# W2's product in the seven-product form, and the weight sums chained by adding DMA transfers

## The chip, the cores and the metric

One core of a Trainium2 chip. The metric is device time in microseconds of one execution; the median of the runs shown counts.

## What is computed

One layer of an encoder over 768 tokens (512 of one request, 256 of the other), in float32: a half-step SwiGLU FFN, a mixer (attention and two-way HGRN2 side by side), and a second half-step FFN, each followed by a residual and a layer norm. The change touches the two FFNs and the loads of weights everywhere.

```python
def swiglu_ffn(x, w13, w2):                    # x 768 x 1024, w13 1024 x 5632, w2 2816 x 1024
    gate, up = jnp.split(x @ w13, 2, axis=-1)
    return (jax.nn.silu(gate) * up) @ w2
...
x = layer_norm(ALPHA * x + 0.5 * swiglu_ffn(x, ffn_w13[l, 0], ffn_w2[l, 0]), ln_g[l, 0], ln_b[l, 0])
```

## The kernel before

**Numbers in two parts.** Every operand of a large product is split into a high part, rounded to the matmul's format by a ScalarE cast (L112), and the rest, by a VectorE subtraction (L113). A product is the sum of three passes, high x high, high x low, low x high (`PASSES`, L144).

**The FFN** runs 11 steps (`ffn`, loop at L504). A step makes two tiles of 128 hidden columns: gate products, up products, SiLU and their product H. W13's products are already in a seven-product form (Strassen-Winograd): activations and weights are cut into 2 x 2 blocks, seven products of block sums replace eight, and sums of the results give the four output blocks. `pair_products` (L371) does the seven products B11, B21, T2, T1, T3, B22, T4 in this order, each 4 x 3 matmuls of 384 columns. The activations' block sums are made once and stay in SBUF (`areaA`, `areaB`); the weights' sums are made for every pair.

**The weights of a pair.** `pair_loads` (L331) loads three blocks in one transfer and two in another, and adds a block A21 onto the latter two by transfers that GpSimd issues with `accum_op=ALU.add` (L340; "adding transfer" here). `pair_weights` (L343) makes two more sums on VectorE (L359) and splits seven blocks into `ring` tiles, of which there are six; so a weight can be split when an earlier product has left its ring tile.

**W2.** Steps 1 to 9 also multiply the H of the step before by two rows of tiles of W2: `group` (L443) takes one token tile and one half of W2's columns, 2 x 3 matmuls of 512 columns into a PSUM tile `pd` (two of them), and VectorE adds the result to the residual `xr` (L452). Twelve such groups are a step's share; `fill` (L510) puts one behind each product from the third on. The last two steps' H goes through `group` after the loop, with the layer norm behind it (`finish`, L533). `w2_units` (L431) loads and splits W2.

**Order.** The framework puts each engine's instructions in order at build time, by the program's order and by when it expects operands, buffers and banks to be ready, and adds the waits. SP issues plain loads, GpSimd adding transfers and a few tiny instructions of the layer norms. Buffers have names with a size and a count (`BUFS`, L77): an allocation waits for an earlier user of the same name.

**First steps.** `first_a` (L550) starts the first FFN from a transposed copy of x, `first_pairs` (L463) the second; both do the first gate pair by plain products and then the first up pair's weights and the activations' sums. `load` and `unit` (L121, L134) load W_in and W_out between the FFNs in tiles of 128 x 1024.

Of the kernel before, what the change touches and what calls it, by code (L numbers as in the profile page):

```python
# [14 lines left out]
P = 128  # L15
# [23 lines left out]
def encoder_layer(ctx: ExitStack, tc: tile.TileContext, a, y_prompt, y_sample):  # L39
# [30 lines left out]
    def area_b(n, dt):  # L70
# [7 lines left out]
            "Dt": (768, 1), "P1": (768, 1), "Ft": (1536, 1), "qt": (768, 1), "nr": (384, 1), "Dc": (192, 1),  # L78
            "xb": (1536, 2)}
# [38 lines left out]
    def raw_tile():  # L118
        return wp.tile([P, 1024], F32, name="raw", tag="raw", bufs=4)

    def load(*srcs):  # L121

        raw = raw_tile()
        if len(srcs[0].shape) == 2:
            nc.sync.dma_start(raw, srcs[0])
            return raw
        r3 = raw.rearrange("p (k c) -> p k c", k=srcs[0].shape[1])
        c0 = 0
        for s in srcs:
            nc.sync.dma_start(r3[:, :, c0:c0 + s.shape[2]], s)  # L130
            c0 += s.shape[2]
        return raw

    def unit(*srcs, hl=None):  # L134

        raw = load(*srcs)
        hl = hl or (ring(), ring())
        split(hl[0], hl[1], raw)
        return hl
# [6 lines left out]
    CHUNK = 8  # L146

# [48 lines left out]
    def constants():  # L196

        k = {}

        rows = raw_tile()[:24, :P]  # L200
# [28 lines left out]
        mraw = raw_tile()  # L229
# [101 lines left out]
    def pair_loads(idx, j):  # L331


        w = a["w13_t"][idx, j]
        base = buf("xb").rearrange("p (b k c) -> p b k c", b=3, k=4)
        nc.sync.dma_start(base, w[:, :3])
        sums = raw_tile().rearrange("p (b k c) -> p b k c", b=2, k=4)
        nc.sync.dma_start(sums, w[:, :2])
        for b in range(2):
            nc.gpsimd.dma_start(sums[:, b], w[:, 3], accum_op=ALU.add)  # L340
        return [base[:, b] for b in range(3)] + [sums[:, b] for b in range(2)]

    def pair_weights(r, slots=()):  # L343


        A22, A11, A12, S1, S3 = r
        slots = list(slots)
        out = []
        S = {}

        def put(src):
            rg = (slots.pop(0) if slots else None) or ring()
            v = rg.rearrange("p (s k c) -> p s k c", s=2, k=4)
            split(v[:, 0], v[:, 1], src)
            out.append(v)

        def add(tag, x, y):
            t_ = buf(tag, n=512).rearrange("p (k c) -> p k c", k=4)
            dve.tensor_tensor(t_, x, y, ALU.add)  # L359
            return t_  # L360

        def s2():
            S[2] = add("Dt", S1, A11)
            put(S[2])

        def s4():
            put(add("P1", S[2], A12))

        return [lambda: put(A11), lambda: put(A12), s2, lambda: put(S1), lambda: put(S3), s4, lambda: put(A22)], out

    def pair_products(ws, C, fill, par):  # L371
# [7 lines left out]
        def product(b, bank, more=False):  # L379
            n = 0  # L380
            tl, off, dist = spot(b)
            for k in range(4):
                for wi, xi in PASSES:
                    pe.matmul(bank, lhsT=ws[b][:, wi, k, :],  # L384
                              rhs=view(tl, off + xi * 512 + k * P, [[dist, 3], [1, P]]),
                              start=n == 0 and not more, stop=n == 11, skip_group_check=True)
                    n += 1
            fill(b)
# [17 lines left out]
    BLOCK = ((1, 2), (3, 0))  # L406
    W2R = ("kc", "kc", "P2", "Xt")
    ORD = (1, 2, 0, 2, 1, 0, 2, 0, 2, 0, 2)

    def ffn(idx, ln_idx, tail, first):  # L410
# [11 lines left out]
        def up_pair(ws, G, hs, fill):  # L422
# [5 lines left out]
            for j in range(2):  # L428
                split(hs[j][:, :T], hs[j][:, T:], H[:, j, :])

        def w2_units(s, last=False):  # L431

            raws = [load(w2[f * P:(f + 1) * P, :]) for f in (2 * s, 2 * s + 1)]
            out = [[], []]
            for c in range(2):
                for j in range(2):
                    rg = buf(W2R[c * 2 + j], F32R, 1024) if not last else \
                        view(B[2], c * 1024, [[1, 1024]]) if j else view(B[1], 3072 + c * 1024, [[1, 1024]])
                    split(rg[:, :512], rg[:, 512:], raws[j][:, c * 512:(c + 1) * 512])
# [15 lines left out]

        def weights(n):

            do, out = pair_weights(pair_loads(idx, (n % 2) * NS + n // 2))
            for f in do:
                f()  # L460
            return out

        def first_pairs(start):  # L463
# [19 lines left out]
            r = [raw_tile().rearrange("p (m k c) -> p m k c", m=2, k=4) for _ in range(2)]  # L483
            for n in range(2):
                for m in range(2):
                    nc.sync.dma_start(r[n][:, m], a["w13_t"][idx, 0][:, BLOCK[m][n]])
            ru = pair_loads(idx, NS)
            for b, raw in zip((B11, B21), r):
                start(b)
                hl.append([ring().rearrange("p (m k c) -> p m k c", m=2, k=4) for _ in range(2)])  # L490
                split(*hl[-1], raw)
            do, ws = pair_weights(ru, [None, None] + [buf(n, F32R, 1024) for n in W2R])
# [5 lines left out]
            for f in (do[0], do[1], sums[0], do[2], sums[1], do[3], sums[2], do[4], do[5], sums[3], do[6]):  # L498
                f()
            return G, ws  # L500

        G, ws = first(idx, NS) if idx == 0 else first_pairs(first)
        w2l = {}
        for s in range(NS):  # L504
            if s > 0:
                w2l[s - 1] = w2_units(s - 1)
                wg, ws = ws, weights(2 * s + 1)
            todo = [(c, t) for c in range(2) for t in range(NT)] if 0 < s < NS - 1 else []

            def fill(n, s=s, todo=todo):  # L510
                if todo and n >= 0:
                    c, t = todo.pop(0)
                    group([2 * s - 2, 2 * s - 1], w2l[s - 1][c], t, c)

            if s > 0:
                G = gate_pair(wg, lambda n: fill(n - 2))
# [8 lines left out]
            up_pair(wu, G, hs, fill)  # L525
# [4 lines left out]
        bc = ln_rows(ln_idx, raw_tile)  # L530
# [19 lines left out]
    def first_a(idx, ns):  # L550
# [14 lines left out]
        ru = pair_loads(idx, ns)  # L565
        nc.sync.dma_start(ident, a["c_ident"])
        for t in range(NT):
            nc.sync.dma_start(xr[:, t, :], x_rows[t])
# [10 lines left out]
        do, ws = pair_weights(ru, [None, None] + [buf(n, F32R, 1024) for n in W2R])  # L579
        for n in range(2):  # L580
# [16 lines left out]
            if n:  # L597
                do[0]()
                do[1]()
            for m in range(2):  # L600
                act.activation(G[:, m, n * 384:(n + 1) * 384], banks[m], AF.Silu)
        b11, b21, b12, b22 = xb

# [9 lines left out]
        do[2]()  # L613
        do[3]()
        sums(T1, b11)
        do[4]()
        sums(T3, b12)
        do[5]()
        do[6]()
# [382 lines left out]
    def out_unit(k, *places):  # L1002
        raw = load(w_out[k * P:(k + 1) * P, :])
        if not isinstance(places[0], list):
            split(places[0], places[1], raw)
            return [[p_[:, c * 512:(c + 1) * 512] for c in range(2)] for p_ in places]
        for c in range(2):
            split(places[0][c], places[1][c], raw[:, c * 512:(c + 1) * 512])
# [136 lines left out]
```

## Time and profile before

| | us |
|---|---|
| median of 3 runs | 1476.99 (1476.22 to 1478.14) |
| the profiled execution | 1475.67 |
| its span, first to last instruction | 1473.7 |
| TensorE, VectorE, ScalarE, GpSimd busy | 1443.5, 954.1, 615.0, 121.5 |

The rows further down are of the profiled execution. PE is TensorE's matmuls, PEld its weight loads, DVE VectorE, ACT ScalarE, POOL GpSimd, SP the engine that issues plain transfers. In a row of a timeline stand start, duration, engine, line, operation, output<-inputs, shapes and count, and in brackets the idle time before it with what ended it. Matmuls overlap, so their pace is read from starts.

### The profile page before, as it was taken

The numbers are of one execution on the slowest core, as the hardware profiler recorded it, in microseconds if no ns is written. First come the engines' busy times: TensorE is split into PE (matmuls) and PEld (weight loads), VectorE is DVE, ScalarE is ACT, GpSimd is POOL, SyncE is SP. The second block draws the span as 40 slices with busy tenths as digits, with TensorE's granted clock in tenths as the row PEclk, the third lists the DMA queues.
The fourth block names the chain that finished last, engine by engine and source line by source line (L and its number), as shares of the span: only waits on it lengthen the run. The fifth ranks groups of instructions, "written<-read, shape, count | busy, mean of one in ns | idle before, by whom it ended". The sixth has DMA issues, their size and how long they took to land.

```text
span 1473.7 us, 23217 instructions
## 1 busy us (share of the span) xinstructions
PE 1443.5 (98%) x9343; PEld 1338.0 (91%) x9343; DVE 954.1 (65%) x1615; ACT 615.0 (42%) x1222; POOL 121.5 (8%) x149
## 2 busy tenths in 40 slices
PE   7999999999999999999999999999999999999996
PEld 6999999999999898999988987899999999999995
DVE  6866566666666768444588736776666666666656
ACT  7533333333333444465664432363333333333341
POOL 1100000000000110000000002120000000000002
PEclk9999999999999999999999999999999999999999
DMA  9543344342442441111111143142443424434212
GB/s 319 156 115 99 95 114 111 98 108 86 115 113 95 126 115 44 58 30 30 44 30 45 32 143 114 43 115 65 115 110 98 109 85 115 112 98 125 67 43 86
DMA packets 67437, 140.80 MB, mean 96 GB/s; under 512 B 13417, under 2 KB 33793, under 8 KB 67329
## 3 DMA queue, kind: packets, MB, share of 16 engines
q1 hardware_dynamic: 55232, 117.29, 23.0%
q0 software_dynamic: 12096, 22.03, 9.6%
q8 instruction: 73, 1.20, 0.3%
q14 instruction: 36, 0.29, 0.1%
HBM read 133.01 MB, written 6.29 MB: 95 GB/s over the span
## 4 chain that ended last, share of the span: by engine, by line
PE 88%; DVE 5%; ACT 2%; DMA 2%; POOL 1%; issue 1%; SPq 0%; DVEq 0%; ACTq 0%; POOLq 0%
PE pa L384 30%; PE pd L448 21%; PE pb L384 12%; PE pa L159 9%; PE ptm L672 4%; PE pwo L1028 4%; PE pp L907 2%; DMA raw<-w_t 1%; PE pav L801 1%; DVE xr L320 1%; DVE Ut L768 1%; PE ps L891 1%; ACT Ft L302 1%; PE ptr L187 1%; PE pp L901 1%
## 5 line engine op out<-in xcount | busy, mean ns | idle before, releaser
L384 PE MATMUL pa<-areaA,ring 128*128 128x384 f32 x1488 | 273.1, 335 | 0.0
L384 PEld LDWEIGHTS pa<-areaA,ring 128*128 128x128 f32 x1488 | 261.0, 188 | 6.0
L448 PE MATMUL pd<-kc,Kt 128*128 128x512 f32 x720 | 185.5, 392 | 0.0
L384 PE MATMUL pa<-areaB,ring 128*128 128x384 f32 x984 | 185.3, 337 | 0.0
L384 PEld LDWEIGHTS pa<-areaB,ring 128*128 128x128 f32 x984 | 174.0, 188 | 6.0
L112 ACT CAST ring<-raw 128x512 fp32r<-128x512 f32 (+2 forms) x116 | 84.6, 731 | 218.7 <-PE pb L384 92.5
L452 DVE SCALAR_TENSOR_TENSOR xr<-pd,xr 128x512 f32<-128x512 f32 x240 | 164.9, 687 | 6.7 <-PE pd L448 6.4
L159 PE MATMUL pa<-areaA,ring 128*128 128x384 f32 x864 | 167.5, 343 | 0.9 <-ACT Kt L691 0.9
L448 PEld LDWEIGHTS pd<-kc,Kt 128*128 128x128 f32 x720 | 133.6, 188 | 21.2
L112 ACT CAST ring<-xb 128x512 fp32r<-128x512 f32 x126 | 77.9, 621 | 176.3 <-PE pa L384 130.1
L159 PEld LDWEIGHTS pa<-areaA,ring 128*128 128x128 f32 x864 | 148.4, 188 | 2.5 <-ACT Kt L691 1.4
L113 DVE TENSOR_TENSOR ring<-xb,ring 128x512 fp32r<-128x512 f32 x126 | 87.6, 698 | 92.7 <-ACT ring L112 90.2
L340 POOL DMA_DIRECT2D raw<-w_t x84 | 74.4, 1038 | 792.4 <-DVE P L359 615.9
L113 DVE TENSOR_TENSOR ring<-raw,ring 128x512 fp32r<-128x512 f32 (+2 forms) x116 | 96.0, 829 | 40.6 <-ACT ring L112 33.8
L448 PE MATMUL pd<-P,Kt 128*128 128x512 f32 x360 | 103.1, 394 | 1.0 <-DVE xr L452 1.0
L448 PE MATMUL pd<-Xt,Kt 128*128 128x512 f32 x360 | 102.4, 392 | 0.0
L384 PE MATMUL pb<-areaB,ring 128*128 128x384 f32 x480 | 91.3, 338 | 0.0
L384 PE MATMUL pb<-areaA,ring 128*128 128x384 f32 x480 | 90.1, 334 | 0.0
L384 PEld LDWEIGHTS pb<-areaB,ring 128*128 128x128 f32 x480 | 85.6, 188 | 3.1
L384 PEld LDWEIGHTS pb<-areaA,ring 128*128 128x128 f32 x480 | 84.5, 188 | 3.4
L672 PE MATMUL ptm<-ring,areaA 128*128 128x256 f32 x576 | 81.7, 289 | 0.0
L448 PEld LDWEIGHTS pd<-Xt,Kt 128*128 128x128 f32 x360 | 67.6, 188 | 15.1
(241 smaller groups left out, 1982.2 us busy)
## 6 DMA issues: line engine op xcount, KB each, us to landing
xb<-w_t SPq DMA_DIRECT2D x42, 768.0 KB, 6.4
raw<-ffn_w SPq DMA_DIRECT2D x44, 512.0 KB, 7.4
raw<-w_t SPq DMA_DIRECT2D x42, 512.0 KB, 3.8
raw<-w_t POOLq DMA_DIRECT2D x84, 256.0 KB, 5.6
raw<-w_in SPq DMA_DIRECT2D x22, 512.0 KB, 3.9
raw<-w_out SPq DMA_DIRECT2D x8, 512.0 KB, 3.4
park<-xr SPq DMA_DIRECT2D x6, 512.0 KB, 3.0
xr<-park SPq DMA_DIRECT2D x6, 512.0 KB, 6.0
```

Of the source, the lines that this page charges most:

```text
L112: act.copy(dst_hi, src)
L113: dve.tensor_tensor(dst_lo, src, dst_hi.bitcast(F32), ALU.subtract)
L159: pe.matmul(pt, lhsT=hl[wi][:, k * P:(k + 1) * P], rhs=tri(g * 2048 + xi * 1024 + k * P), start=n == 0, stop=n == 3 * KT - 1)
L187: pe.transpose(pt[:, k * P:(k + 1) * P], src[:, k * P:(k + 1) * P], ident)
L302: act.activation(junk[c], x[c], AF.Square, bias=nm, accum_out=w[:, 2 + c:3 + c])
L340: nc.gpsimd.dma_start(sums[:, b], w[:, 3], accum_op=ALU.add)
L384: pe.matmul(bank, lhsT=ws[b][:, wi, k, :], rhs=view(tl, off + xi * 512 + k * P, [[dist, 3], [1, P]]), start=n == 0 and not more, stop=n == ...
L448: pe.matmul(pd, lhsT=hT[f][:, hi * T + t * P:hi * T + (t + 1) * P], rhs=w[wi], start=n == 0, stop=n == tot - 1)
L452: dve.scalar_tensor_tensor(xs, pd, 0.5, xs, ALU.mult, ALU.add, accum_out=total)
L672: pe.matmul(pt, lhsT=xT(t, xi, k), rhs=w[k // 4][wi][:, k % 4, :], start=n == 0, stop=n == 3 * KT - 1)
L907: pe.matmul(pp[j][:, 384:448], lhsT=PTs[j % 2][:, i * P:(i + 1) * P], rhs=V[:, kb0 + i, kv * 64:kv * 64 + 64], start=i == 0, stop=i == nk - 1)
L1028: pe.matmul(po[c], lhsT=cat(t, xi, k), rhs=wo[k][wi][c], start=k == 0 and n == 0, stop=k == KT - 1 and n == 2)
```

## The change

For steps 1 to 9 of each FFN the product of H and W2 takes the seven-product form too. H's two tiles and two halves of the tokens are its 2 x 2 blocks, so a product is one block of 128 hidden columns by 384 tokens, times a block of 128 rows and 512 columns of W2 (or sums of such). `h_form` makes H's sums on VectorE (three instructions) and splits seven blocks. `form_groups` runs the products token tile by token tile, three matmuls each. Products of one chain accumulate in the same PSUM tile, and after each the tile is added to or subtracted from the part of `xr` to which its running sum belongs. The 21 groups of a step are taken from `SEQUENCE` behind the products of W13 by the counts in `FILLS`.

Weights of all forms, W13's and W2's, are loaded in blocks of 128 x 512 (`block`, 15 of them, in place of `raw` and `xb`). One sum (S1) is made by an adding transfer at once. The others come one after the other in the block X: it is split as A11, then a transfer adds A21 and it is split as T3, then A22 for T2, then A12 for B22. Only the first up pair of each FFN makes these three on VectorE (`by_dma=False`). The order of the weights of a pair is B11, T3, B21, T2, T1, B22, T4.

Besides: W_in and W_out are loaded and split in two halves; the layer norm's rows go to `Ut` tiles; in `first_a` the first weights are loaded into `xr` and the rows of x after them.

```diff
-            "xb": (1536, 2)}
...
+    BLOCKS = 15
...
+    def form_loads(A11, A12, A21, A22):
+        out = []
+        for src in (A11, A22, A12, A22):
+            t_ = block()
+            nc.sync.dma_start(t_, src)
+            out.append(t_)
+        nc.gpsimd.dma_start(out[1], A21, accum_op=ALU.add)
+        return out, (A21, A22, A12)
+
+    def form_weights(loaded, place, by_dma=True):
+        (X, S1, A12, A22), more = loaded
+        out = [None] * 7
+        def put(n, src):
+            rg = place(n)
+            out[n] = rg[:, :512], rg[:, 512:1024]
+            split(*out[n], src)
+        def thunk(n, src, then=None):
+            def f():
+                put(n, src)
+                if then is not None and by_dma:
+                    nc.gpsimd.dma_start(X, more[then], accum_op=ALU.add)
+            return f
...
+        if by_dma:
+            return {n: thunk(n, src, then) for n, src, then in (
+                (B11, X, 0), (T3, X, 1), (B21, A12, None), (T2, X, 2), (T1, S1, None), (B22, X, None),
+                (T4, A22, None))}, out
+        R = block()
+        nc.sync.dma_start(R, more[0])
...
-        return [lambda: put(A11), lambda: put(A12), s2, lambda: put(S1), lambda: put(S3), s4, lambda: put(A22)], out
...
+    FILLS = (0, 0, 1, 2, 2, 2, 2, 2, 2, 2, 2, 2, 1, 1)
...
+        def h_form(H, G, hs):
...
+            base(B11, 0, 0)
+            dve.tensor_tensor(view(G, 0, [[384, 2], [1, 384]]), view(H, 0, [[1152, 2], [1, 384]]),
+                              view(H, 384, [[0, 2], [1, 384]]), ALU.subtract)
+            dve.scalar_tensor_tensor(G[:, 1, :384], G[:, 0, :384], -1.0, H[:, 1, 384:], ALU.mult, ALU.subtract)
+            dve.scalar_tensor_tensor(G[:, 1, 384:], G[:, 1, :384], -1.0, H[:, 1, :384], ALU.mult, ALU.subtract)
+            sums((T2, T4), buf("Dt", F32R), buf("P1", F32R), G[:, 1, :])
+            ft = buf("Ft", F32R)
+            sums((T1, T3), ft[:, :T], ft[:, T:], G[:, 0, :])
+            base(B21, 1, 0)
+            base(B22, 1, 1)
...
+        W2AT = {B11: "kc", T2: "kc", T3: "P2", T4: "Xt", B21: "kc", T1: "kc", B22: "P2"}
+        C11, C12, C21, C22 = (0, 0, 0.5), (0, 1, 0.5), (1, 0, -0.5), (1, 1, -0.5)
+        CHAINS = ([(B11, [C11]), (T2, [C12]), (T3, [C22]), (T4, [C21])],
+                  [(T1, [C22]), (B22, [C12])], [(B21, [C11])])
+        SEQUENCE = [(0, i, n) for n in range(4) for i in range(2)] + [(0, 2, n) for n in range(4)] + \
+                   [(1, i, n) for n in range(2) for i in range(2)] + [(1, 2, n) for n in range(2)] + \
+                   [(2, i, 0) for i in range(3)]
+        def form_groups(h, do, ws):
+            banks = {}
+            def group(c, i, n):
+                b, outs = CHAINS[c][n]
+                for need in (T3, b) if b == T2 else (b,):
+                    if ws[need] is None:
+                        do[need]()
+                if n == 0:
+                    banks[c, i] = psd("pd")
+                pd = banks[c, i]
+                for m, (hi, wi) in enumerate(PASSES):
+                    pe.matmul(pd, lhsT=h[b][hi][:, i * P:(i + 1) * P], rhs=ws[b][wi],
+                              start=n == 0 and m == 0, stop=m == 2, skip_group_check=True)
+                for half, tok, sign in outs:
+                    xs = xr[:, tok * 3 + i, half * 512:(half + 1) * 512]
+                    dve.scalar_tensor_tensor(xs, pd, sign, xs, ALU.mult, ALU.add)
...
+        ORDER = (B11, T3, B21, T2, T1, B22, T4)
...
             if s > 0:
-                w2l[s - 1] = w2_units(s - 1)
                 wg, ws = ws, weights(2 * s + 1)
...
+                if s < NS - 1:
+                    todo += form_groups(hf, *form_weights(w2_loads(s - 1), lambda b: buf(W2AT[b], F32R, 1024)))
...
-        bc = ln_rows(ln_idx, raw_tile)
+        bc = ln_rows(ln_idx, lambda: buf("Ut", n=1024))
...
-        rw = [raw_tile().rearrange("p (m k c) -> p m k c", m=2, k=4) for _ in range(2)]
+        rw = [xr[:, n, :].rearrange("p (m k c) -> p m k c", m=2, k=4) for n in range(2)]
```

## Rows read from the trace of the kernel before

**Rows 1.** The page's parts 1 and 4: busy us per engine, shares of the chain.

```profile
PE 1443.5 (98%) x9343; PEld 1338.0 (91%) x9343; DVE 954.1 (65%) x1615; ACT 615.0 (42%) x1222; POOL 121.5 (8%) x149
...
PE 88%; DVE 5%; ACT 2%; DMA 2%; POOL 1%; issue 1%; SPq 0%; DVEq 0%; ACTq 0%; POOLq 0%
```

**Rows 2.** Windows: length; PE, PEld, DVE, ACT, POOL busy; clock, DMA share, GB/s.

```profile
223.10:269.02 45.92, 45.92 (x242) 42.86 (x241) 29.25 (x46) 16.30 (x29) 3.54 (x4) 1.00 0.37 103
1024.36:1070.28 45.92, 45.92 (x242) 42.87 (x241) 29.25 (x46) 16.30 (x29) 3.52 (x4) 1.00 0.37 104
```

**Rows 3.** Timeline of TensorE inside one step.

```profile
241.03 2.24 PE L384 MATMUL pa<-areaB,ring 128*128 128x384 f32 x12
243.11 1.55 PE L448 MATMUL pd<-kc,Kt 128*128 128x512 f32 x6
244.51 2.29 PE L384 MATMUL pb<-areaB,ring 128*128 128x384 f32 x12
```

**Rows 4.** Timeline of TensorE in step 1 of the first FFN.

```profile
52.07 0.39 PE L448 MATMUL pd<-kc,Kt 128*128 128x512 f32 x1
52.30 0.87 PE L384 MATMUL pb<-areaA,ring 128*128 128x384 f32 x4
53.01 0.90 PE L448 MATMUL pd<-kc,Kt 128*128 128x512 f32 x3
```

**Rows 5.** Groups by shape in the step 223.10 to 269.02: busy us, mean ns, idle.

```profile
L452 DVE SCALAR_TENSOR_TENSOR xr<-pd,xr 128x512 f32<-128x512 f32 x12 | 8.3, 688 | 0.0
...
L113 DVE TENSOR_TENSOR Kt<-Ut,Kt 128x768 fp32r<-128x768 f32 x2 | 1.8, 950 | 0.0
L359 DVE TENSOR_TENSOR Dt<-raw,xb 128x512 f32<-128x512 f32 x2 | 1.4, 693 | 0.1
...
L112 ACT CAST kc<-raw 128x512 fp32r<-128x512 f32 x2 | 1.1, 624 | 0.0
...
L426 DVE SCALAR_TENSOR_TENSOR Ut<-Ut 128x384 f32<-128x384 f32 x2 | 1.1, 552 | 0.0
```

**Rows 6.** Timeline of VectorE in the same step.

```profile
240.55 0.69 DVE L113 TENSOR_TENSOR ring<-Dt,ring 128x512 fp32r<-128x512 f32 x1 [2.10 <-ACT ring L112]
...
255.77 1.28 DVE L113 TENSOR_TENSOR kc<-raw,kc 128x512 fp32r<-128x512 f32 x2
```

**Rows 7.** Timeline of TensorE in the last FFN's tail.

```profile
1453.36 0.99 PE L448 MATMUL pd<-P,Kt 128*128 128x512 f32 x3 [0.44 <-DVE xr L452]
```

**Rows 8.** The page's parts 3 and 6: queues (share of 16 engines), one issue.

```profile
q1 hardware_dynamic: 55232, 117.29, 23.0%
q0 software_dynamic: 12096, 22.03, 9.6%
...
raw<-ln_g SPq DMA_DIRECT2D x2, 512.0 KB, 5.0
```

**Rows 9.** Line L340, the adding transfers: issue ns min/median/max, then landing.

```profile
L340 POOL DMA_DIRECT2D raw<-w_t x84: 853/962/1252, 20.1 to 1375.7; - x84
...
DMA to landing us min/median/max: 4.1/5.6/10.5
```

**Rows 10.** DMA view of the first 45 us: share by slice, adding transfers (median).

```profile
DMA  0166898999999999999999999999999298818992
...
raw<-w_t POOLq DMA_DIRECT2D x4, 256.0 KB, 6.9
```

**Rows 11.** Timeline of the first up pair.

```profile
28.55 0.69 DVE L359 TENSOR_TENSOR Dt<-raw,xb 128x512 f32<-128x512 f32 x1 [3.19 <-DMA raw<-w_t]
...
33.87 3.75 PE L384 MATMUL pa<-areaA,kc 128*128 128x384 f32 x12 [2.95 <-ACT nr L391]
```

**Rows 12.** The window from 33.87, columns as in rows 2.

```profile
33.87:39.50 5.63, 5.63 (x23) 5.63 (x24) 5.63 (x8) 4.65 (x7) 1.75 (x2) 0.70 0.77 169
```

**Rows 13.** Timeline of VectorE in the last tail.

```profile
1429.26 1.83 DVE L113 TENSOR_TENSOR areaB<-Ut,areaB 128x768 fp32r<-128x768 f32 x2
...
1436.28 1.29 DVE L320 SCALAR_TENSOR_TENSOR xr<-xr,ln,raw 128x1024 f32<-128x1024 f32 x1 [1.73 <-ACT Ft L302]
```

**Rows 14.** Groups by shape of the whole run: splits of the two sizes.

```profile
L113 DVE TENSOR_TENSOR ring<-raw,ring 128x512 fp32r<-128x512 f32 x83 | 57.3, 691 | 7.7 <-ACT ring L112 1.1
L113 DVE TENSOR_TENSOR ring<-raw,ring 128x1024 fp32r<-128x1024 f32 x31 | 37.8, 1222 | 28.9 <-ACT ring L112 28.6
```

More of the change, by code (lines that the diff above doesn't have):

```diff
@@ L116, in ring, with block, halves_of @@
         return wp.tile([P, 1024], F32R, name="ring", tag="ring", bufs=6)
[L118 to L132, printed above, removed]
+    def block():
+        return wp.tile([P, 512], F32, name="block", tag="block", bufs=BLOCKS)
+    def halves_of(*srcs):
+        out = []
+        for n in range(2):
+            raw = block()
+            out.append(raw)
+            if len(srcs[0].shape) == 2:
+                nc.sync.dma_start(raw, srcs[0][:, n * 512:(n + 1) * 512])
+                continue
+            kn = srcs[0].shape[1] // 2
+            r3 = raw.rearrange("p (k c) -> p k c", k=kn)
+            c0 = 0
+            for s in srcs:
+                nc.sync.dma_start(r3[:, :, c0:c0 + s.shape[2]], s[:, n * kn:(n + 1) * kn])
+                c0 += s.shape[2]
+        return out
     def unit(*srcs, hl=None):
-        raw = load(*srcs)
+        raws = halves_of(*srcs)
         hl = hl or (ring(), ring())
-        split(hl[0], hl[1], raw)
+        for n, raw in enumerate(raws):
+            split(hl[0][:, n * 512:(n + 1) * 512], hl[1][:, n * 512:(n + 1) * 512], raw)
         return hl
@@ L198, in constants @@
         k = {}
-        rows = raw_tile()[:24, :P]
+        rows = block()[:24, :P]
         nc.sync.dma_start(rows[0:4, :], a["attn_norm_g"][0].rearrange("(j p) -> j p", p=P))
@@ L329, in ln_rows @@
         return out
-    def pair_loads(idx, j):
[L334 to L367, printed above, removed]
-        return [lambda: put(A11), lambda: put(A12), s2, lambda: put(S1), lambda: put(S3), s4, lambda: put(A22)], out
@@ new lines, in form_loads, with late, f, third @@
+    def form_loads(A11, A12, A21, A22):
+        out = []
+        for src in (A11, A22, A12, A22):
[17 more added lines that the diff above has]
+            return f
+        def late(n, extra):
+            def f():
+                dve.tensor_tensor(X, X, extra, ALU.add)
+                put(n, X)
+            return f
+        if by_dma:
[4 more added lines that the diff above has]
+        nc.sync.dma_start(R, more[0])
+        def third():
+            dve.tensor_tensor(R, X, R, ALU.add)
+            put(T3, R)
+        def second():
+            dve.tensor_tensor(X, R, A22, ALU.add)
+            put(T2, X)
+        return {B11: thunk(B11, X), B21: thunk(B21, A12), T3: third, T2: second, T1: thunk(T1, S1),
+                B22: late(B22, A12), T4: thunk(T4, A22)}, out
@@ L427, in up_pair, with base, sums @@
             dve.scalar_tensor_tensor(H[:, 1, :384], C21, -1.0, G[:, 1, :384], ALU.mult, ALU.mult)
-            for j in range(2):
-                split(hs[j][:, :T], hs[j][:, T:], H[:, j, :])
+            if not form:
+                for j in range(2):
+                    split(hs[j][:, :T], hs[j][:, T:], H[:, j, :])
+                return None
+            return h_form(H, G, hs)
+        def h_form(H, G, hs):
+            out = {}
+            flat, free = view(H, 0, [[1, 2 * T]]), view(G, 0, [[1, 2 * T]])
+            def base(b, j, n):
+                c = slice(n * 384, (n + 1) * 384)
+                out[b] = hs[j][:, c], hs[j][:, T + n * 384:T + (n + 1) * 384]
+                split(*out[b], H[:, j, c])
+            def sums(blocks, hi, lo, src):
+                split(hi, lo, src)
+                for n, b in enumerate(blocks):
+                    out[b] = hi[:, n * 384:(n + 1) * 384], lo[:, n * 384:(n + 1) * 384]
+            base(B11, 0, 0)
[8 more added lines that the diff above has]
+            base(B22, 1, 1)
+            return out
@@ L497, in first_pairs, with fill @@
             sums = form_sums()
-            for f in (do[0], do[1], sums[0], do[2], sums[1], do[3], sums[2], do[4], do[5], sums[3], do[6]):
+            for f in (do[B11], do[B21], do[T3], sums[0], do[T2], sums[1], do[T1], sums[2], do[B22], sums[3],
+                      do[T4]):
                 f()
             return G, ws
-        G, ws = first(idx, NS) if idx == 0 else first_pairs(first)
+        G, ws = first(idx, first_weights) if idx == 0 else first_pairs(first)
         w2l = {}
+        todo, hf = [], None
         for s in range(NS):
             if s > 0:
-                w2l[s - 1] = w2_units(s - 1)
                 wg, ws = ws, weights(2 * s + 1)
[L508 to L513, printed above, removed]
+                if s < NS - 1:
+                    todo += form_groups(hf, *form_weights(w2_loads(s - 1), lambda b: buf(W2AT[b], F32R, 1024)))
+                else:
+                    w2l[s - 1] = w2_units(s - 1)
+            def fill(n):
+                for _ in range(FILLS[n] if todo else 0):
+                    todo.pop(0)()
             if s > 0:
-                G = gate_pair(wg, lambda n: fill(n - 2))
+                G = gate_pair(wg, fill)
             if s < NS - 1:
@@ L602, in first_a @@
         b11, b21, b12, b22 = xb
+        for t in range(NT):
+            nc.sync.dma_start(xr[:, t, :], x_rows[t])
         def sums(b, src):
```

72 lines of the change are left out of this document (41 added, 31 removed).

## The prediction

> **What bounds the kernel now.** I read the page's busy times and chain first [rows 1]: TensorE is busy for 98% of the span, and 88% of the chain that ended last is matmuls. Then the table of windows [rows 2]. Nine middle steps of each FFN repeat exactly: two of the 18 are shown, each 45.92 us long with TensorE busy for all 45.92, VectorE for 29.25 and ScalarE for 16.30, at full granted clock. So the steps hold 18 x 45.92 = 827 us of the span, and in them a matmul that goes away gives back its time for as long as nothing else becomes late. The reader should look in [rows 3] at starts, not durations: twelve 384-column matmuls of one product take 2.08 us (241.03 to 243.11, 173 ns each), and a group of six 512-column matmuls of W2 takes 1.40 us (243.11 to 244.51, 233 ns each). A step is 14 products and 12 groups: 14 x 2.085 + 72 x 0.233 = 46.0, which is the window.
>
> TensorE's queue doesn't follow the program's order blindly: in [rows 4] matmuls of a W2 group (pd) and of a product (pb) alternate in pieces of one to four. The instructions were put in order at build time by what was expected to be ready. A queue is then kept in that order on the chip, so a wait that is longer than expected holds everything behind it.
>
> **The change, part by part.**
>
> **TensorE.** The W2 part of a step had 2 halves of the columns x 6 token tiles x 6 matmuls = 72. It gets 7 products x 3 token tiles x 3 passes = 63, of the same shape. Nine fewer at 0.233 us is 2.10 us a step, 43.8 us a step, and over 18 steps **-37.7 us**. The weight loads fall by the same nine. Nothing else on TensorE changes.
>
> **VectorE per step**, by durations of [rows 5]. Removed: four sums at L359 (4 x 0.69 = 2.8). Added: 9 more evictions, since the 21 groups are each read once (12 before; 9 x 0.69 = 6.2); 3 more splits of W2 blocks (7 instead of 4, 3 x 0.69 = 2.1); for the hidden block three sums (one of 768 columns at 0.95, two of 384 at 0.55) and five splits (two at 0.95, three at 0.55) in place of two at 0.95: 5.6 - 1.9 = 3.7. Sum 29.25 - 2.8 + 6.2 + 2.1 + 3.7 = 38.4 of 43.8 us. Where instructions follow each other closely one costs less than its duration: two of 512 columns take 1.28 together, not 1.38 [rows 6], so the need is nearer 34 if packed. VectorE goes from 64% to 78-88% and is still not the bound. But it waits in order: in [rows 6] it sits 2.10 us on a split whose ScalarE cast waits for a ring slot, and an eviction stands behind. Today TensorE doesn't notice.
>
> **ScalarE** gains 3 casts (0.62) and about 1.5 us in the hidden block's casts: 16.3 to about 20 us of 43.8. Not a bound, but a cast that waits for a late adding transfer holds the copies L391 to L397 behind it, and these free the bank into which the next product accumulates.
>
> **Banks.** A chain of one token tile accumulates on in the same bank after each eviction, so the next group of that chain waits for it. Two chains are interleaved, but the four groups of the third token tile (0,2) follow each other alone, and FILLS puts two of them, T2 and T3, behind one product. Its price is bounded by 0 (the build-time order puts pieces of the next product between, as in [rows 4]) and by an eviction of 0.69 plus the 0.44 that TensorE waited for one where it had nothing else [rows 7]: 1.1 us a step. I take 0.4, nearer to the row of the steps: **+7 us**.
>
> **Adding transfers.** A step has 4 now (2 a pair) and gets 12: four for each of two weight pairs and four for W2, three of the four in a chain on one block: split, add the next operand, split, add. Issue costs GpSimd about 1 us each [rows 9], 12 of 43.8, on a queue with nothing else in the steps. The load: 84 of them take 9.6% of the span of all 16 engines, 1.68 us each; the plain loads 117.29 MB in 23.0%, 2.9 us per MB [rows 8]. A step's plain loads go from 3.67 MB (2 x 1280 + 1024 KB) to 3.15 MB (12 x 256 KB), so it goes from 4 x 1.68 + 3.67 x 2.9 = 17.4 (the windows say 0.37 x 45.92 = 17.0 [rows 2]) to 12 x 1.68 + 3.15 x 2.9 = 29.3 of 43.8: a share of 0.67. There is room. SP issues 12 blocks a step instead of 6 transfers, on a queue that holds nothing else in the steps.
>
> Do the chains arrive? From issue to landing such a transfer takes 4.1 to 10.5 us, median 5.6 [rows 9]; in the first 45 us, where the DMA engines are busy for about 0.9 of the time, the median is 6.9 [rows 10]. A link is cast and subtract (1.4) plus landing (5.6) = 7.0 us. In a pair of 21.9 us the six ring slots give the next B11 its place after the second product (6.3 us); T3 can be split at 13.3, T2 at 20.3, done at 21.7. T2 is read 28.2 us after the pair's start: 6.5 us to spare over two links. W2 is tighter: its B11 needs a kc slot that the group T1 of the last token tile frees, some 9 us before the step ends. T3 is then split about 2 us before the step, T2 5.1 after it, done at 6.5; its group stands behind the fourth product, at 9.7. To spare: 3.2 us over two links, so it holds up to a landing of 5.6 + 1.6 = **7.2 us**. Beyond that a step loses 2 us per us. Bounds: 0 at 6.9 or less, and at 10.5 2 x 3.3 = 6.6 us a step, +119 us. I take 0, nearest to the median under the heavy load.
>
> The Trainium skill (DMA: Bandwidth & Descriptors, Anatomy of one DMA - SWDGE (gpsimd) path) gives about 2.0 us plus bytes/436e3 us for such a transfer, an estimate of 2.6 us for 256 KB. The rows say 5.6 and decide; by the page's figure the W2 chain would have 9 us to spare and the rival below would have no ground.
>
> The same page (Measured (HBM→SBUF, 128 partitions, SWDGE, issued from GpSimd)) advises at least 1 MiB per transfer; this change goes the other way, from 512 and 768 KB to 256 KB. By its efficiencies loads would take more of the DMA engines' time than my 2.9 us per MB, which uses up room, not time, as long as the share stays under 1.
>
> **The start.** Now the second pair's T2 weights wait for an adding transfer: VectorE sits 3.19 us for it, TensorE then 2.95 [rows 11], and the stretch that follows the idle time ran at a granted clock of 0.70, part of it at the lower level, 1.2 GHz of 2.4 [rows 12]. In the change T3, T2 and B22 of the first pair are made from loaded blocks by VectorE (3 sums instead of 2), and only T1 needs an adding transfer, one product later. Best case: the idle 2.95 goes, and of the slow product the 3.75 - 2.08 over its usual time: -5; worst: loads of x, issued later, hold scale_residual: +3. VectorE is busy for most of this stretch anyway, so **-2 us**.
>
> **Tails.** The LN rows go to Ut, free only when H is split (about 1431), instead of an earlier block; with 5 us to land [rows 8] they come at about 1436, where ln_apply starts now (1436.28 [rows 13]). 0 to +2 us for each FFN: **+1**. **Between the FFNs** a 1024-column split (1.22) becomes two of 0.69, on engines that don't bound there [rows 14]; more blocks let loads run ahead: -1 to +1, taken as 0.
>
> Sum against the profiled run, 1475.67 (span 1473.7, 2.0 around it): 1475.7 - 37.7 + 7 - 2 + 1 = 1444.0. The median shown is 1476.99, 1.3 above that run, so **1445**.
>
> **The rivals.**
>
> *The eviction waits are paid.* If the build-time order doesn't fill the gap, or VectorE's fuller queue delays evictions elsewhere too, each step pays 1.1 us and some: 18 x 1.1 = 20 instead of 7, 1458; with twice that 1478. For it: VectorE's in-order wait and its 78-88%. Against it: TensorE's order is interleaved already [rows 4].
>
> *The chained transfers are late; slower than before.* One mechanism: W2's T2 block, two links behind B11's split, in every step; TensorE's queue stands at that group. It decides from a landing of 7.2 us, and cancels the whole gain at 7.2 + 2.10/2 = 8.25 us. At 9 us a step loses 3.6: 18 x (3.6 - 2.1) = +27, about 1504. For it: the DMA share nearly doubles, and landings up to 10.5 exist; if the build-time order expected shorter transfers than these, casts are queued too early and hold ScalarE as well. Against it: 6.9 us where the DMA engines were fuller than they'd be here.
>
> *It doesn't shorten the path:* the saved matmuls come back as other waits, some 2.1 us a step, within 0.2% of before.
>
> **How the numbers follow.** Forecast 0.50 (its own range 1432 to 1452: no stalls and -5 at the start, to 0.8 us a step); eviction waits 0.20 (1452 to 1473); chain late 0.25 (over 1480); nothing 0.05. A measurement of this kernel can tell about 0.2%, 3 us, from no change. Faster 0.70, same 0.05, slower 0.25. The range leaves out 0.02 below and the later part of the late chain (landings over 8.9 us): 1432 to 1500.
>
> **What would show it.** Right: steps of about 44 us, 63 matmuls at the new W2 line with 233 ns between starts, TensorE without idle time in the steps, landings of adding transfers under 7 us, no 2.95 us gap near 31 us. Wrong: idle time of TensorE before the T2 group behind a cast that waits for DMA (the chain), or before the third tile's T3 group behind an eviction (the banks); VectorE near 100% of a step; the granted clock below full in the steps.

## The result: 9.2% slower

| | before | after | ratio |
|---|---|---|---|
| median, us | 1477.01 | 1612.52 (1609.57 to 1614.7) | 1.092 [1.089, 1.094] |
| span of the profiled run, us | 1473.7 | 1609.2 | |

The forecast was 1445, with 1500 as the upper end of its range. The profile of the changed kernel: its page's busy times, which answer to [rows 1], and two windows, which answer to [rows 2]: one step of the first FFN and a stretch over the eight middle steps of the second.

```profile
PE 1458.4 (91%) x9181; PEld 1320.3 (82%) x9181; DVE 1074.3 (67%) x1895; ACT 672.6 (42%) x1364; POOL 251.2 (16%) x299
...
168.30:220.71 52.41, 46.68 (x232) 41.91 (x230) 35.75 (x59) 19.05 (x36) 10.22 (x12) 0.97 0.57 121
...
1112.00:1530.00 418.00, 373.75 (x1897) 335.94 (x1896) 295.63 (x486) 159.33 (x288) 81.60 (x94) 1.00 0.56 120
```

The matmuls are as forecast, 162 fewer. But TensorE, busy for all 45.92 us of a step before, now idles 5.7 us of 52.4, and no engine is near full: VectorE 35.75, ScalarE 19.05. From one up pair's multiply (line L425, now L452) to the next, the 135.5 us of span are gained and lost so: up to the first -3.5, the first steps of the FFNs +23.5 and +9.8, their eight middle steps +50.4 and +41.5, their last steps +6.2 and +5.1, between the FFNs +2.8, after the last multiply -0.2. So it is in the steps. The waits of ScalarE, VectorE and TensorE (us in total, times, longest), and how long the chained transfers took, which answers to [rows 9]:

```profile
ACT ring L111 <- DMA block<-w_t: 306.3, 109, 6.1
...
DVE ring L112 <- ACT ring L111: 297.6, 131, 6.5
...
PE pd L516 <- DVE xr L520: 88.5, 73, 3.0
PE pa L409 <- ACT nr L416: 19.2, 17, 3.3
...
PE pa L409 <- ACT ring L111: 4.4, 2, 3.8
...
DMA to landing us min/median/max: 3.9/4.3/6.6
```

This is a chain to be read downwards: casts wait for adding transfers, splits on VectorE wait for these casts, and TensorE waits for evictions that stand behind the splits, or for copies behind the casts. Only the last of the TensorE rows is a wait for a weight itself: twice, in the first FFN's first step. The same chain in one step, from the timelines of the four engines (start, duration; the wait before it and its releaser in brackets):

```profile
215.57 4.35 PE L409 MATMUL pa<-areaA,ring 128*128 128x384 f32 x24
...
221.29 0.62 ACT L111 CAST ring<-block 128x512 fp32r<-128x512 f32 x1
...
223.24 0.68 DVE L112 TENSOR_TENSOR ring<-block,ring 128x512 fp32r<-128x512 f32 x1
...
224.29 0.86 POOL L364 DMA_DIRECT2D block<-w_t  x1 [3.36 <-DVE ring L112]
...
228.54 1.15 ACT L111 CAST ring<-block 128x512 fp32r<-128x512 f32 x2 [2.15 <-DMA block<-w_t]
...
229.19 1.30 DVE L112 TENSOR_TENSOR ring<-block,ring 128x512 fp32r<-128x512 f32 x2 [1.90 <-ACT ring L111]
230.41 0.68 DVE L520 SCALAR_TENSOR_TENSOR xr<-pd,xr 128x512 f32<-128x512 f32 x1
...
231.14 0.98 PE L516 MATMUL pd<-P,Ft 128*128 128x512 f32 x3 [1.08 <-DVE xr L520]
...
235.15 1.14 ACT L111 CAST ring<-block 128x512 fp32r<-128x512 f32 x2 [2.98 <-DMA block<-w_t]
...
235.81 0.69 DVE L112 TENSOR_TENSOR ring<-block,ring 128x512 fp32r<-128x512 f32 x1 [2.96 <-ACT ring L111]
...
242.00 0.62 ACT L111 CAST ring<-block 128x512 fp32r<-128x512 f32 x1 [4.16 <-PE pa L409]
...
244.60 1.22 PE L516 MATMUL pd<-kc,Dt 128*128 128x512 f32 x2 [2.62 <-DVE xr L520]
...
250.96 2.27 PE L409 MATMUL pa<-areaA,ring 128*128 128x384 f32 x12
```

B11's cast at 221.29, its split, the next summand at 224.29; T3's cast stands waiting until 228.54, behind it a split, behind that the eviction at 230.41, for which TensorE waits 1.08 us. T2's cast stands waiting until 235.15 in the same way. B22's starts at 242.00, 0.10 us behind the landing of its transfer (at 241.90; the profile names a product that ended at the same time), and behind it TensorE waits 2.62 us for an eviction. Yet the product that reads T2 begins at 250.96: its weights were done at 236.50, 14.5 us before they were read. No weight was late here; the casts stood in ScalarE's queue too early, where they held all that came behind.

Of the 35 links of the pairs issued from 150 to 450 us, each took 0.36 us from the split's end to the issue in the median and 4.50 (4.04 to 5.59) to the landing, and **each of the 35 casts started 0.08 to 0.10 us behind its landing**: not one came later than its data.

### The profile page after: what moved, and what is told of

Its sections match the earlier page's. It is cut to its first block, busy times and chain, and to the rows that moved or that the text cites. A ratio compares the mean times of both kernels' runs of the same rounds, so it can differ in the third digit from the quotient of the medians.

```text
span 1609.2 us, 24155 instructions
## 1 busy us (share of the span) xinstructions
PE 1458.4 (91%) x9181; PEld 1320.3 (82%) x9181; DVE 1074.3 (67%) x1895; ACT 672.6 (42%) x1364; POOL 251.2 (16%) x299
## 5 line engine op out<-in xcount | busy, mean ns | idle before, releaser
L112 DVE TENSOR_TENSOR ring<-block,ring 128x512 fp32r<-128x512 f32 x348 | 235.6, 688 | 296.4 <-ACT ring L111 292.2
L111 ACT CAST ring<-block 128x512 fp32r<-128x512 f32 x348 | 208.7, 619 | 380.5 <-DMA block<-w_t 306.3
L409 PE MATMUL pa<-areaA,ring 128*128 128x384 f32 x1488 | 294.7, 347 | 23.8 <-ACT nr L416 19.2
L520 DVE SCALAR_TENSOR_TENSOR xr<-pd,xr 128x512 f32<-128x512 f32 x378 | 251.2, 685 | 36.9 <-PE pd L516 35.4
L364 POOL DMA_DIRECT2D block<-w_t x120 | 103.9, 866 | 549.9 <-DVE ring L112 508.4
L516 PE MATMUL pd<-kc,Kt 128*128 128x512 f32 x324 | 93.0, 395 | 1.3 <-DVE xr L520 1.3
L516 PE MATMUL pd<-kc,Dt 128*128 128x512 f32 x108 | 38.4, 434 | 44.3 <-DVE xr L520 42.7
L111 ACT CAST kc<-block 128x512 fp32r<-128x512 f32 x80 | 49.5, 618 | 65.5 <-PE pd L516 42.3
L777 PEld LDWEIGHTS ptm<-ring,areaA 128*128 128x128 f32 x576 | 72.8, 190 | 0.5
L516 PE MATMUL pd<-P,Ft 128*128 128x512 f32 x162 | 49.7, 416 | 22.2 <-DVE xr L520 22.2
L516 PEld LDWEIGHTS pd<-kc,Kt 128*128 128x128 f32 x324 | 59.1, 188 | 11.1 <-DVE xr L520 3.0
L345 POOL DMA_DIRECT2D block<-w_t x42 | 39.8, 948 | 171.1 <-DMA block<-w_t 101.5
```

Of the source, the lines that this page charges most:

```text
L111: act.copy(dst_hi, src)
L112: dve.tensor_tensor(dst_lo, src, dst_hi.bitcast(F32), ALU.subtract)
L345: nc.gpsimd.dma_start(out[1], A21, accum_op=ALU.add)
L364: nc.gpsimd.dma_start(X, more[then], accum_op=ALU.add)
L409: pe.matmul(bank, lhsT=ws[b][wi][:, k * P:(k + 1) * P], rhs=view(tl, off + xi * 512 + k * P, [[dist, 3], [1, P]]), start=n == 0 and not mo ...
L516: pe.matmul(pd, lhsT=h[b][hi][:, i * P:(i + 1) * P], rhs=ws[b][wi], start=n == 0 and m == 0, stop=m == 2, skip_group_check=True)
```

## The experiments

The theory: the casts of chained sums stand in ScalarE's queue ahead of their landings, and hold copies, splits and, through VectorE, evictions. The rivals: the 21 evictions in two banks behind a fuller VectorE cost it; or the load of the transfers; or late data. TensorE's idle time (span less busy) is the telling column; it was 30 us in the kernel before. A time is one execution, except for the change and e5 (four each, the median) and e7 (two). The runs with sums left out, or sent to no reader, do not compute the layer.

| run | pairs' sums | W2's sums | TensorE idle | time |
|---|---|---|---|---|
| after | chained | chained | 151 | 1612.52 |
| e1 | chained, other order | chained | 169 | 1637.4 |
| e9 | chained | immediate | 177 | 1648.63 |
| e3 | chained | old form | 113 | 1599.05 |
| e4 | immediate | chained | 101 | 1549.24 |
| e2 | left out | chained | 53 | 1479.5 |
| e6 | to no reader | chained | 80 | 1522.0 |
| e14 | to no reader | immediate | 43 | 1462.01 |
| e2b | left out | left out | 35 | 1445.93 |
| e5 | immediate | immediate | 37 | 1450.97 |
| e11 | immediate | chained, late | 45 | 1465.32 |
| e7, e8, e12, e15 | chained, late | e7 chained, else immediate | 181, 86, 108, 49 | 1652.49, 1519.36, 1566.84, 1470.52 |
| e13, e16 | chained, late | chained, late | 91, 63 | 1536.78, 1495.83 |

The kernel before took 1477 to 1478.5 beside them.

**Leaving parts out.** Another order, the pairs' chain left out, the old W2, and mixed sums:

```
-        ORDER = (B11, T3, B21, T2, T1, B22, T4)
+        ORDER = (B11, B21, T3, T1, T2, T4, B22)
```


> Only the order in which a pair's weights are made changes: B11, B21, T3, T1, T2, T4, B22, so that one other weight, and with it one more ring slot (a product later), stands between two links of the chain. Theory 1 (the casts of the pairs' chained sums stand in ScalarE's queue ahead of the landing of their adding transfers, about 4.3 us after issue, and hold VectorE and the evictions behind): ScalarE's 306 us of waits on block<-w_t fall by more than half, the steps go from 51.7 us to 44-47, the run to 1450-1520. Theory 2 (the 21 evictions, two banks and a fuller VectorE cost the 8 us by themselves): steps stay at 50 or more, run 1585-1615.

```
-                if then is not None and by_dma:
+                if then is not None and by_dma and chained:
```


> Leaves out the three chained adding transfers of every pair of W13 after the first of each FFN (T3, T2 and B22 are split from A11 alone, so these sums are not computed); the transfer that makes S1 and all of W2's chain stay. Theory 1: ScalarE waits for block<-w_t by under 40 us, the 11th step, which has no W2 products, returns from 37-38 us to 31.9, the steps go to 44-46, the run to 1440-1475. Theory 2: the 11th step returns all the same, the others stay at 49 or more, run 1570-1600.

```
-                if s < NS - 1:
-                    todo += form_groups(hf, ...)
+                w2l[s - 1] = w2_units(s - 1)
```


> W2 goes back to twelve groups of six matmuls in a step, one behind each product from the third on; the pairs' chained sums stay as in the change. Theory 1: still slow, the pairs' chain costs each of the 20 steps 4-6 us, as in the 11th step, so 50-52 us a step and 1560-1595 in all. Theory 2: steps near 46, run 1470-1490.

```
+        S3 = block()
+        nc.sync.dma_start(S3, more[1])
+        nc.gpsimd.dma_start(S3, more[0], accum_op=ALU.add)
...
+        return {B11: put(B11, X), B21: put(B21, A12), T2: put(T2, X, S1), T1: put(T1, S1), T3: put(T3, S3),
+                B22: put(B22, X, A12), T4: put(T4, A22)}, out
```


> The pairs' sums are made as in the kernel before: two adding transfers at once (S1, S3) and two sums on VectorE, in the order B11, B21, T2, T1, T3, B22, T4; W2 keeps the seven products with its chain. VectorE gets 2.8 us a step more than in the change. Theory 1: steps at 44-47, run 1445-1500. Theory 2: steps at 50 or more and VectorE's waits replaced by work, run 1580-1620.

Measured: 1637.4, 1479.5, 1599.05, 1549.24. By the theory's ranges e2 and e3 end some 4 us too high, and e1 and e4 are misses. The pairs' chain is worth 133 us beside W2's chain (e2). With the old W2 the kernel is still 121 us above the kernel before (e3; the loads differ too), so W2's form isn't the cause. The other order missed: it doesn't change that the casts stand ahead (0.10 us behind the landing in the median, as in the change). e4 missed too, since W2's own chain does the same. Its row in TensorE's timeline, with ScalarE's above it:

```profile
253.60 0.62 ACT L111 CAST kc<-block 128x512 fp32r<-128x512 f32 x1 [2.25 <-DMA block<-ffn_w]
...
254.65 0.47 ACT L436 COPY nr<-pa 128x384 f32<-128x384 f32 x1
...
255.17 3.25 PE L429 MATMUL pa<-areaA,ring 128*128 128x384 f32 x12 [3.20 <-ACT nr L436]
```

A cast of W2 that the queue reached 2.25 us early holds the copy that frees a product's bank, and TensorE waits 3.20.

**No chain at all.** First without the sums (the edit of e2 for W2 as well), then with all of them by immediate transfers and VectorE (e4's edit for W2 as well).

> The chained adding transfers of the pairs and of W2 are all left out (the T3, T2 and B22 weights are split from the first block as it is, so these sums are not computed; S1's transfers stay); W2 keeps its seven products, 21 evictions and 7 splits. Beside the run without the pairs' chain (1479.5, steps of 45.5 us) it shows what W2's own chain costs. If casts that stand in ScalarE's queue ahead of a landing are the cause, what is left of the 1.5 us a step goes too: 1448 to 1468. If the evictions and the two banks cost it: 1474 to 1485, as with W2's chain.

> No chain anywhere: S1 and S3 of each pair and of W2 by one adding transfer each, issued with the loads, T2 and B22 by a sum on VectorE (six sums a step, 4.1 us more than in the change; VectorE about 42 us of a step of 44 to 46 by durations, less packed). If held casts are the cause, there are none left but the sums stand in VectorE's queue: 1450 to 1490, below the 1549 of the run with W2's chain alone. If the evictions behind a fuller VectorE are the cause, it is slower than that run: 1550 to 1600.

Measured: 1445.93 and 1448.97, each just under its range. A step of e2b, and of e5 (in the repeat of it below):

```profile
135.30:179.40 44.10, 44.10 (x233) 41.16 (x232) 36.13 (x60) 19.51 (x35) 2.59 (x3) 1.00 0.36 90
```

```profile
223.60:267.80 44.20, 44.20 (x233) 41.01 (x232) 39.46 (x66) 19.62 (x35) 5.06 (x6) 1.00 0.51 125
```

TensorE is busy throughout again, with 21 evictions in two banks, and with VectorE at 39.46 of 44.20 us. Evictions, banks and a full VectorE cost at most 0.3 us a step (44.2 against 43.9 by the pace of the matmuls). Against e2b the change has the same 9181 matmuls and 165.1 us more of span: 115.8 of it TensorE's idle time (150.8 against 35.0), 49.3 longer matmuls (1458.4 against 1409.1), about half of it by a lower clock (last section).

**Load without waits.** The pairs' chained transfers issued behind the same splits into blocks that nobody reads:

```
-                    nc.gpsimd.dma_start(X, more[then], accum_op=ALU.add)
+                    to = X if chained else apart[:, then % 2 * 512:(then % 2 + 1) * 512]
+                    moved = nc.gpsimd.dma_start(to, more[then], accum_op=ALU.add)
```


> The pairs' three chained transfers stay in number, kind and size, each issued behind the same split as in the change, but into two blocks that nobody reads, so no cast waits for them (these sums are not computed; 13 blocks in place of 15 make the room). W2's chain and all else as in the change. If held casts are the cause, it runs like the kernel without these transfers: 1472 to 1500. If the load of the adding transfers on the DMA engines or on GpSimd's queue is the cause: 1560 to 1615, as the change.

> The pairs' chained transfers issued behind the same splits into blocks that nobody reads (these sums are not computed), and W2's sums by immediate transfers and VectorE, so that no cast waits for a link at all. If the load costs only by what it does to waiting casts: 1446 to 1458. If it costs by itself: 1480 or more, as the 42 us that it cost beside W2's chain.

Measured: 1522.0 and 1462.01, each between the two ranges expected. The load costs 11 us where no link is waited for (e14 against e5, which has VectorE's sums besides), and 42 where W2's chain is (e6 against e2): there W2's links land after 4.9 us in the median instead of 4.4, and ScalarE's casts of W2 wait for them 132 us in all instead of 59. So the load by itself is a small part; beside a chain that is waited for it is a third of the 133 us, and the longer waits go with it. What the two blocks fewer do in e6 and e14 wasn't tested alone.

**The same chain beside W2 without one.** e4's edit for W2 alone:

> The same kernel, but the pairs' splits placed as in the change. If casts queued ahead of their landings are the cause: 1550 to 1590, about 120 above the kernel without chains (1449), as the same chain cost beside the old form of W2 (1599 against 1477). If the two chains cost only together (load, GpSimd's queue): 1449 to 1490.

Measured: 1648.63, slower than expected by any theory: the pairs' chain alone costs 198 us over e5, W2's alone 98 (e4), both together 162, so the costs don't add up. TensorE waits longer for evictions here than in the change (125.4 us against 88.5):

```profile
PE pd L539 <- DVE xr L543: 125.4, 73, 4.6
```

That VectorE's added sums, which stand behind the waiting casts as well, make the 36 us over the change is likely but not shown.

**All the work, other places.** If the place in the queue is the cause, the chains must get cheap when each split is emitted, and its cast kept in ScalarE's order, some three products behind the link before it. First for pairs, W2's as they came:

```
+        PLACE = ((B11, 1), (B21, 3), (T3, 4), (T1, 5), (T2, 8), (T4, 8), (B22, 11))
...
+            late.extend((done[0] + at, do[b]) for b, at in PLACE)
...
+            tc.keep_in_program_order(act.copy(out[n][0], src))
```


> All the work and all the transfers of the change, sums too, but the splits of the next pair are placed one by one behind the products of the running pair (B11 behind the first, T3 behind the fourth, T2 behind the seventh, B22 behind the third of its own pair), and kept in that place in ScalarE's queue, so that each link of the chain has three products, some 9 us, to land before its cast's turn comes. If casts that stand ahead of the landing are the cause: steps of 44 to 46 us, 1448 to 1490. If the data itself is late, or the load costs it: over 1580.

Measured: 1652.49, a plain miss, in the rivals' range. Most of the pairs' casts now came behind their landings, but 45 still waited for them (109 in the change). W2's stood at theirs, and there the data really were late: links landed after 6.5 us in the median, and TensorE waited 95.7 us for T2's cast.

```profile
ACT ring L358 <- DMA block<-w_t: 128.1, 45, 8.0
...
PE pd L517 <- ACT kc L358: 95.7, 18, 6.5
```

So W2's chain was taken out (e8), or alone placed late (e11):

> The pairs' sums by chained transfers, all of them, with their splits placed late as in the run of late casts (there the pairs' casts came 5 us after their landings, but W2's came at them); W2's sums by immediate transfers and VectorE, so that no cast of W2 waits. If casts that are queued ahead of their landings are the cost of a chain, the pairs' chain is now free: 1446 to 1475. If the chain costs by its load or by late data: 1530 to 1600.

```
+    FILLS = (0, 0, 0, 1, 1, 0, 2, 2, 2, 3, 3, 3, 2, 2)
...
+                if todo and n in (2, 5):
+                    w2do[T3 if n == 2 else T2]()
```


> W2's chain with the pairs' sums by immediate transfers and VectorE, the kernel that took 1549.24; now the split of W2's T3 weights is placed behind the first product's copy of the step and that of T2 behind the fourth's, each some three products after the link before it, and the groups of T2 and after come later to match (FILLS). If casts queued ahead of their landings are the cause: 1447 to 1480. If W2's chain costs by late data or load: 1530 or more.

Measured: 1519.36 (e9, the same work: 1648.63) and 1465.32 (e4: 1549.24). The places alone (in e11 those of W2's groups too) give back 129 and 84 us. e8 missed its range: in the step that its trace was read for, two casts are still early, T3's by 2.92 us and, by the order of the casts, B22's by 2.43. Two attempts at that, the second of which also moved B22:

```
+        PLACE = ((B11, 0), (B21, 3), (T1, 4), (T3, 5), (T2, 8), (T4, 8), (B22, 11))
```


> As the late pairs' run (1519.36), but B11's split one product earlier and T3's one place later, so that the one cast a step that still waited 2.9 us for its landing comes after it. If held casts are all of a chain's cost: 1449 to 1475. If something of the chain costs apart from them: over 1495.

```
+        PLACE = ((B11, 1), (B21, 3), (T1, 4), (T3, 5), (T2, 8), (T4, 8), (B22, 12))
```


> As the late pairs' run (1519.36), with the split of T3 one product later (it waited 2.9 us a step for its landing) and that of B22 one later too. If a chain is free where no cast waits for its landing: 1449 to 1475. If the pairs' chain keeps costing some 70 us wherever its casts stand: 1500 or more.

Measured: 1566.84, in the rival's range, and 1470.52. In e12 TensorE's build-time order drew the third and fourth products together, so their two copies ended at once and the queue came to B22's cast a product sooner:

```profile
1149.12 0.48 ACT L441 COPY qt<-pa 128x384 f32<-128x384 f32 x1 [3.22 <-PE pa L430]
1149.58 0.48 ACT L443 COPY qt<-pb 128x384 f32<-128x384 f32 x1
1154.17 1.66 ACT L358 CAST ring<-block 128x512 fp32r<-128x512 f32 x3 [4.11 <-DMA block<-w_t]
...
1156.77 1.22 PE L540 MATMUL pd<-kc,Dt 128*128 128x512 f32 x2 [3.76 <-DVE xr L544]
```

One cast that waits 4.11 us costs the step 6.8 (51.0 against 44.2). With B22 one product later (e15, where B11 too is back at its place of e8) this loss is gone, and the steps are 44.3 to 45.9 us. Yet ScalarE's casts wait for the pairs' landings about as long in all three: 107.9 us (e8), 93.9 (e12) and 98.2 (e15). It is not the wait of the cast that costs, but what stands behind it. Then the whole change, with all its sums and transfers, and only the places different (W2's as in e11):

> All sums by chained transfers, as in the change, the same transfers and the same 63 matmuls a step; the pairs' splits placed as in e12, W2's as in the run with W2's late chain (1465). If held casts are the cause of the change's loss: 1455 to 1500, near the forecast. If the load or the length of two chains together is the cause: 1540 or more.

> As e15 with W2's sums chained too, its splits placed as in the run of W2's late chain: all the work and all the transfers of the change. If held casts are the cause: 1460 to 1500. If two chains cost together whatever the places: 1530 or more, as the first attempt at this (1537).

Measured: 1536.78 with e12's places, a miss, and 1495.83 with e15's, within the range. So 117 of the 167 us that the change loses against e2b come back by order alone. Casts still wait in e16, 186 us of ScalarE's time (354 in the change), but little that TensorE needs stands behind them: it waits 9.0 us for evictions and 1.3 for a copy `nr`, where the change waited 88.5 and 19.2.

```profile
PE pd L519 <- DVE xr L523: 9.0, 10, 5.1
```

**The version without chains, timed.**

> The kernel without chains that took 1448.97, timed against the kernel before in three rounds: 1447 to 1451, 1.8 to 2.0% below it.

Measured: 1450.97 (1450.6 to 1452.82), ratio 0.9825 [0.9809, 0.9841]: 26 us below the kernel before, with the change's seven-product W2, and near the 1445 that was forecast for the change.

## Why the prediction was wrong

- **TensorE, -37.7 us: right.** Nine fewer matmuls a step; 44.1 us a step in e2b against 43.8 forecast. (From multiply to multiply eight steps of each FFN, not nine, have 45.92 us in the kernel before; the first with W2 has 39.4 and 43.1. The sum goes by matmuls and stands.)
- **VectorE 34 to 38.4, ScalarE about 20 us a step: right**, 35.75 and 19.05. That VectorE isn't the bound: right, up to 39.46 (e5).
- **Banks and evictions, 0.4 us a step: right in size**, 0.2 to 0.3 in e2b (44.1 against 14 x 2.085 + 63 x 0.233 = 43.9). The rival of the eviction waits falls with it: TensorE does wait 88.5 us for evictions, but they are late because of the casts, and without chains those waits are gone.
- **The load: a share of 0.67 was forecast**; it is 0.57 in the longer step and 0.68 in e16's of 45 us. That there is room: right but for some 11 us (e14).
- **The landing: 5.6 us was taken, 4.3 measured** (W2's links 4.1, the pairs' 4.5 in the stretch above), better than forecast and far under the 7.2 from which the slow rival was to decide. By the Trainium skill (DMA: Bandwidth & Descriptors, Anatomy of one DMA - SWDGE (gpsimd) path) an estimate gave 2.6 us; the shortest chained transfer of the change took 3.9, and no run here shows one near 2.6.
- **"6.5 us to spare over two links", the cost of the chains taken as 0: this step failed.** Its times were right: it has T3 and T2 split 13.3 and 20.3 us after the pair's start, and in the step shown their casts start 13.0 and 19.6 behind its first product (215.57), each as its data land. The data had even more to spare, 14.5 us. But time to spare of the data costs nothing only if the instruction that waits for it stands that late in its queue. The prediction had the mechanism in two places: a cast that waits holds the copies behind it, and, in the rival's last line, that the build-time order may queue casts too early. It gave neither a price. The rows had one: in the only place of the kernel before where a sum was read soon after its issue, VectorE stood 3.19 us ahead of the landing and TensorE then 2.95 [rows 11]. Nine links a step at 3.19 us each are an estimate of the upper bound, 28.7 us a step, where the prediction took 0; the change lost 8.3 against e2b in the step of 52.41.
- **The slow rival had the right sign and the wrong mechanism.** It waited for W2's T2 block to be late, from a landing of 7.2 us. In the change TensorE waited for the cast of that block once, 1.6 us, and for a pair's ring tile twice, 4.4 us, all in the first steps of the FFNs. In e7 T2's block was late in every step, at landings of 6.5 us, below the rival's 7.2, with the splits in other places.
- **The start, -2: not confirmed.** The first multiply comes 3.5 us earlier, but TensorE has done 175 matmuls by then where it had done 201, so the 3.5 are no gain. The idle time near 31 us that was to go is still there, 3.04 us in front of a product at 34.93, for the cast of T2's weights, which are now made from loaded blocks.
- **The tails, +1: -0.2. Between the FFNs, 0: +2.8.**

What stays open: whether all chains can be placed without loss. e16 keeps 45 us over e5; its transfers land later (W2's 5.8 us in the median, the pairs' 5.0), and no run tells whether better places would give back the rest.

## What to carry to other kernels

Cost a wait on an in-order queue by what stands behind the waiting instruction, not by how early its data are for their reader; where the order is fixed at build time, look for the one place where it already met such a wait, and multiply for an upper bound. A sum in a chain of transfers ties each link to two engines' queues; immediate transfers into separate blocks and two more sums on an engine with room gave the same result with no wait, and turned 9% slower into 1.8% faster. When an order is mended by hand, look at the trace after each move: one cast placed right put another in front of its landing.

## What the runs showed of the hardware that was not expected

How much an idle stretch costs beyond itself. In e12 TensorE, at full clock before, stood 3.76 us at 1153.01; the window before it, and the two after it, of 6 and 12 matmuls:

```profile
1150.77:1153.01 2.24, 2.24 (x13) 1.92 (x11) 0.00 (x0) 0.00 (x0) 0.00 (x0) 1.00 0.92 214
1156.77:1159.49 2.72, 2.72 (x6) 2.15 (x7) 2.30 (x4) 0.52 (x1) 0.76 (x1) 0.50 0.52 175
1159.49:1163.07 3.58, 3.58 (x13) 3.57 (x12) 0.69 (x1) 0.00 (x0) 0.97 (x2) 0.54 0.72 116
```

The granted clock is at its lower level, 1.2 of 2.4 GHz, in the first of these two and nearly all of the second: the 6 matmuls take 2.72 us in place of 1.40 and the 12 take 3.58 in place of 2.09, 2.8 us more, and with the 3.76 that makes 6.6 of the 6.8 us by which the step is longer. In the change itself the window behind a wait of 2.62 us has 0.61:

```profile
244.60:248.28 3.68, 3.68 (x12) 3.39 (x13) 2.48 (x4) 0.62 (x1) 0.00 (x0) 0.61 0.99 251
```

Not every wait does this: behind the 1.08 us at 231.14 the granted clock stays at 1.00.

So 49 of the 165 us that the change lost against e2b are not idle time at all, but the same matmuls taking longer. The lower clock is about half of that: the mean granted clock is 0.981 in the change and 0.996 in e2b, which makes 1609.2 x 0.019 - 1444.1 x 0.004 = 25 us, an estimate. The rest fits the restarts, also an estimate: TensorE begins again after a wait 117 times in the change and 23 times in e2b, and three matmuls of W2 begun after a wait at full clock take 0.98 us (the row at 231.14) in place of 0.70 by the pace, so 94 x 0.28 = 26 us.
